# Gate products in chunks of 512, 512 and 152 columns, dt weights' two parts side by side, sample state products in four row groups

## The chip, the cores and the metric

The kernel runs on one core of a Trainium2 chip. The metric is the device time of one execution in microseconds. Engines are named as in the profile: PE is TensorE (PEld its weight loads), DVE is VectorE, ACT is ScalarE, POOL is GpSimd, SP is SyncE, which issues the transfers. TensorE multiplies a moving operand by a stationary one of up to 128 x 128 (the contraction lies on the partitions) into PSUM; the other engines evict from there.

## The reference

One inference step of a small hybrid network, in fp32, for 1024 frames of a new stream (the prompt) and 16 frames each of 8 running streams (the samples), 1152 tokens with 1024 features:

```python
def trunk(x, ...):               # for each layer, with norms before and after each part
    # layer 0: RG-LRU             layer 1: Mamba-2 SSD            each followed by SwiGLU
def rglru_mixer(...):
    r = sigmoid(xc @ w_r + b_r)  # four blocks of 256 x 256, after a causal convolution
    i = sigmoid(xc @ w_i + b_i)
def ssd_mixer(...):
    proj = h @ w_in              # z (2048), x (2048), B (512), C (512), dt (32)
    dt = softplus(dt_raw + dt_bias)
def ssd_scan(...):               # by chunk c, group g (4), head r (8 in a group)
    states = einsum('bcjgn,bcjgrp->bcgrpn', B, xdt * decay)
    s = s * exp(acs[-1]) + states
```

Outputs are the features of all tokens and the new states: of the convolutions, of the RG-LRU, and of the SSD (for each of 8 samples and 32 heads a 64 x 128 matrix).

## The kernel before, in words

**Layout.** Features lie on the partitions and tokens in the free dimension. Tokens go in three blocks of 384 (`TB`); the last holds 256 prompt tokens and the 128 sample tokens. Weights come in units of 128 x 1024 floats (`wr`), each of which is split into a rounded high part `wh` (a cast on ScalarE to the reduced format float32r) and the rest `wl` (a subtraction on VectorE); activations are split likewise (`hl` holds both parts). A product (`mm3`, line 418) is then three float32r matmuls: high by high, high by low, low by high. `gemm` (line 424) makes 8 x 3 of them for one unit and one token block into one PSUM buffer `mm`.

**Gates.** `gate` in `lru` (line 661 on) multiplies the convolved rows, 1176 columns with the padding of the samples, by a 256 x 256 block of gate weights, for r and for i. Each row of results is made in three chunks of `QC` = 392 columns, 6 matmuls each, and evicted by a sigmoid on ScalarE.

**dt.** The dt unit has 32 weight columns, the rest of its 128 are zero. `dt_tb` (line 837) makes an ordinary gemm for each block and keeps 32 rows of it (`dtr`). `dt_prep` transposes these 32 rows in nine pieces of 128 tokens on TensorE against the identity, and goes on to the decays.

**Scan.** `core` (line 898) is a generator: for each of four groups it goes through eight prompt chunks of 128 tokens and then, as a ninth, the 128 sample tokens (`smp`). A chunk loads its columns of x, B and C (`core<-xbc`) and its cumulated decays, broadcast to all partitions (`core<-acd`), transposes x and B on TensorE into `aux` and `one`, weights the results (`xdt`, `xw`), makes decay matrices on GpSimd, ScalarE and VectorE, then the outputs `py` (eight 64-row products and eight more with the state, profile rows `aux<-core,core 128*64`), and the state's increment. For the samples eight states `sb` are read in, used by eight column-tiled products (`aux<-sb,core 128*32`), and renewed. For each sample b this is: a mask of B's 128 tokens with the 16 of the sample (`bm`, on VectorE), a full product bm x xw of 128 x 512 in plain fp32 (two instructions), `sb` times its decay on GpSimd, the addition of the product on VectorE, and a transfer out.

**What sets the order.** Every operation is first recorded by a `Recorder` in program order. It works out the latest start of each operation for a TensorE without pauses, and emits all with priorities by it; the framework's scheduler then lays out each engine's instructions by these priorities and its own estimates. One rule is added (`emit`, line 319): buffers of one kind (a tag) are taken in program order, "slot order". So a PSUM buffer that is written later in the program cannot be taken before one that is written earlier. There are four buffers of the tag `mm`, three of `aux` and one of `one`; SBUF has three of `tmp` and 17 of `row`. The scan's steps are called from between the gemms of the SSD layer (`advance`, with `RATE` 0.4: one chunk for 2.5 gemms) in the order x0 x1 x2 z0 x3 z1 z2 z3. In `core` before the change no operation uses an `mm` buffer.

All recorded instructions have line L332 in the profile, since the recorder emits them there; L335 of the changed kernel is the same line.

Of the kernel before, what the change touches and what calls it, by code (L numbers as in the profile page):

```python
# [8 lines left out]
F32 = mybir.dt.float32  # L9
# [13 lines left out]
QC = NQ // 3  # L23
# [94 lines left out]
for _n, _w in [("ident", 128), ("U", 128), ("Ub", 128), ("ones", 1), ("sm", 8)]:  # L118
    CS[_n] = (_o, _o + _w)
    _o += _w  # L120
NCS = _o

# [6 lines left out]
def lay_inputs(w):  # L129
    w = {k: np.asarray(v) for k, v in w.items()}  # L130
    x = np.concatenate([w["x_prompt"].reshape(SEQ, D), w["x_sample"].reshape(NS * LS, D)], axis=0)
    xt = np.ascontiguousarray(x.T).reshape(KD, P, T).transpose(1, 0, 2)
    wu = np.stack([lay_unit(d, w) for d in plan()])
    pv = np.zeros((P, NPV), np.float32)

    def put(n, a):
        pv[:, PV[n][0]:PV[n][1]] = a

    put("g", np.concatenate([fm(w[n][l]) for l in range(2) for n in
                             ("norm_mix_pre", "norm_mix_post", "norm_ffn_pre", "norm_ffn_post")], axis=1))  # L140
    put("lcw", fm(w["lru_conv_w"][0].T))
    put("lcb", fm(w["lru_conv_b"][0]))
    put("lbr", fm(w["lru_b_r"][0].reshape(-1)))
    put("lbi", fm(w["lru_b_i"][0].reshape(-1)))
    put("lam", fm(w["lru_lambda"][0]))
    put("lh", fm(w["state_lru_h"][0].T))
    put("scw", fm(w["ssd_conv_w"][0].T))
    put("scb", fm(w["ssd_conv_b"][0]))
    put("sd", fm(np.repeat(w["ssd_d"][0], HD)))
    put("sng", fm(w["ssd_norm"][0]))  # L150
    put("dtb", np.broadcast_to(w["ssd_dt_bias"][0], (P, NH)))
    put("alog", np.broadcast_to(w["ssd_a_log"][0], (P, NH)))
    i = np.arange(P)
    same = i[:, None] // LS == i[None, :] // LS
    up = i[:, None] <= i[None, :]
    cs = np.concatenate([np.eye(P), up, up & same, np.ones((P, 1)),
                         i[:, None] // LS == np.arange(NS)[None, :]], axis=1).astype(np.float32)
    scs = fm(w["state_ssd_conv"][0].transpose(2, 0, 1)).reshape(P, 24, 24).transpose(1, 0, 2)
    lcs = w["state_lru_conv"][0].transpose(2, 0, 1).reshape(KD, P, 24)
    s0 = w["state_ssd"][0].reshape(NS, NG, HPG * HD, NST).transpose(1, 0, 3, 2)  # L160
    return {k: np.ascontiguousarray(v) for k, v in
            dict(xt=xt, wu=wu, pv=pv, cs=cs, lcs=lcs, scs=scs, s0=s0).items()}
# [36 lines left out]
def box(a):  # L199
    """The part of its tensor that an access covers: a range of each dimension (all of it where unclear)."""  # L200
# [23 lines left out]
class Recorder:  # L224
    """Collects the instructions of a program, so that each can be issued with a priority that
    follows from when the tensor engine needs its result."""
# [42 lines left out]
    def latest_starts(self, slots):  # L269
        """When each instruction has to start at the latest for the tensor engine to run without a pause."""  # L270
# [73 lines left out]
class Trunk:  # L344
# [57 lines left out]
    def prepare(self, prep):  # L402
        nc = self.nc
        while self.n_prep < min(self.n_raw, self.n_take + prep):
            r = self.raws.pop(self.n_prep)
            h, l = self.get(self.wp, "wh", 1024, F32R, "wh"), self.get(self.wp, "wl", 1024, F32R, "wl")
            nc.scalar.copy(h, r)
            (nc.gpsimd if 1 < self.n_prep < 4 else nc.vector).tensor_tensor(out=l, in0=r, in1=h.bitcast(F32), op=SUB)
            self.preps[self.n_prep] = (h, l)
            self.n_prep += 1  # L410
# [22 lines left out]
    def split_k(self, hl, k, src, scale=None):  # L433
        """hi and lo parts of a source (times a gain per feature): hi + lo is exact."""
# [16 lines left out]
    def sumsq(self, srcs, tag, engine=None, tail=0, square=None):  # L451
        """Sum of the squares of the features, in 1 + tail parts that the tensor engine adds."""
# [23 lines left out]
    def rstd_bc(self, parts, n, tag, tail=0):  # L476
        """1 / sqrt(sum over features / n + eps) of each token, on all partitions."""
# [36 lines left out]
    def store_x(self, tb, k, xt, dst):  # L514
        """Stores the tiles up to k that fill a row."""
        if k % 3 == 2 or k == KD - 1:
            n = k % 3 + 1
            self.nc.sync.dma_start(dst[:, k + 1 - n:k + 1, tb * TB:(tb + 1) * TB],
                                   xt[k // 3][:, :n * TB].rearrange("p (k t) -> p k t", k=n))
# [4 lines left out]
    def pre_rstd(self, tb, s, tail=0):  # L524
        """1/rms of each token before a mixer: it scales the products of the unnormalised x."""
# [5 lines left out]
    def boundary(self, tb, rows, xin, gpost, gpre, xout):  # L531
        """x += norm(mixer output), and what the next mixer takes of it."""
# [34 lines left out]
    def scaled(self, out, ps, tb, lo=0, hi=TB):  # L567
        """Products times 1/rms of their tokens."""
# [61 lines left out]
    def lru(self, hn, xt):  # L630
# [31 lines left out]
        def gate(w, k):  # L662
# [5 lines left out]
            for j, m in enumerate(ms):  # L668
                r[m], i[m] = self.row(s="r"), self.row(s="i")
                for dst, o, b in ((r[m], 0, "lbr"), (i[m], 256, "lbi")):  # L670
                    for c in range(3):
                        ps = self.psm()
                        cc = slice(c * QC, (c + 1) * QC)
                        for q in range(2):
                            ws = slice(q * 512 + o + j * P, q * 512 + o + (j + 1) * P)
                            self.mm3(ps[:, :QC], wh[:, ws], wl[:, ws], xch[2 * k + q][:, cc], xcl[2 * k + q][:, cc],
                                     q == 0, q == 1)
                        order.append(A.activation(dst[:, cc], ps[:, :QC], AF.Sigmoid, bias=self.pv(b, m)))
# [158 lines left out]
    def dt_tb(self, w, hn, tb):  # L837
        if tb == 0:
            self.dtr = self.row(s="dtr")
        ps = self.gemm(w, hn[tb])  # L840
        self.scaled(self.dtr[:NH, tb * TB:(tb + 1) * TB], ps[:NH], tb)

    def dt_prep(self):
# [3 lines left out]
        pt = self.psx()  # L847
        for c in range(NT):
            nc.tensor.transpose(pt[:, c * NH:(c + 1) * NH], raw[:NH, c * P:(c + 1) * P], self.ident[:NH, :NH])
# [48 lines left out]
    def core(self, g, q5, rows):  # L898
# [5 lines left out]
        for c in range(NT):  # L904
# [11 lines left out]
            # token-major copies  # L916
# [16 lines left out]
            # decay matrices  # L933
# [24 lines left out]
            # outputs, feature-major  # L958
# [23 lines left out]
            # states  # L982
# [14 lines left out]
            else:  # L997
                for b in range(NS):
                    bm = self.tmp(P, s="bm")
                    V.tensor_scalar(out=bm, in0=btok, scalar1=self.cst("sm")[:, b:b + 1], scalar2=None, op0=MUL)  # L1000
                    pst = self.psx()
                    M.matmul(pst, bm, xw, start=True, stop=True)
                    o = b * NH + g * HPG
                    G.tensor_tensor(out=v3(sb[b]), in0=v3(sb[b]),
                                    in1=bds[:, o:o + HPG].unsqueeze(2).to_broadcast([P, HPG, HD]), op=MUL)
                    V.tensor_tensor(out=sb[b], in0=sb[b], in1=pst, op=ADD)
                    nc.sync.dma_start(self.o["ss"][g, b], sb[b])
            yield

    def ssd(self, hn, xin, xout):  # L1010
# [26 lines left out]
        def advance(n, ready):  # L1037
            """Goes on with the scan: the outputs of a chunk, and the preparation of the next."""
# [11 lines left out]
        def zs(g):  # L1050
            """Gating and norm of a group."""
# [59 lines left out]
        # output projection, half of the inner width at a time  # L1111
# [25 lines left out]
    def run(self):  # L1137
        nc = self.nc
        self.pvt = self.cp.tile([P, NPV], F32, tag="pv", name="pvt")
        self.cs = self.cp.tile([P, NCS], F32, tag="cs", name="cs")  # L1140
# [27 lines left out]
        nc.sync.dma_start(self.cs, self.i["cs"])  # L1168
# [30 lines left out]
```

## Time and profile before

| what | value |
|---|---|
| median of the runs (lowest to highest of 3) | 3118.02 us (3117.15 to 3123.07) |
| span of the profiled execution (no time of its own is listed) | 3121.6 us |
| mean granted TensorE clock | 0.981 |
| TensorE busy | 3004.5 us, 96%, 17659 instructions |
| VectorE, ScalarE, GpSimd busy | 1734.4, 1010.2 and 466.3 us |
| gate matmuls, 392 columns, three groups of 96 | 34.5 + 34.0 + 33.7 us busy |
| sample state products, 64 instructions | 34.7 us busy |
| longest wait of TensorE | 14.89 us, at 1288.73 us, on VectorE's `rs` |

The RG-LRU layer takes the span's first 446 us, the first SwiGLU runs to about 1290, the SSD layer to about 2200, the second SwiGLU to the end. A row of the timeline gives start, duration, engine, line, operation, written and read tile, shapes and count, and in brackets the idle time of the engine before it with what ended it. In a row of groups the shape behind a tile's names is the stationary operand's and then the moving one's. Durations of matmuls overlap: the next starts before the last has ended, so that TensorE's time for one is read from start to start.

### The profile page before, as it was taken

Reading aid. Unit: us, or ns where it says so; the run is one execution under the profiler, and the core shown is the slowest. Engines: PE = TensorE matmul, PEld = TensorE weight load, DVE = VectorE, ACT = ScalarE, POOL = GpSimd, SP = SyncE. Lnnn points to the kernel's source line nnn. Section 1 sums busy time; section 2 is a strip of 40 time slices with the busy share of each in tenths; the row PEclk is TensorE's granted clock in tenths of the full one; section 3 lists DMA queues with packets and bytes.
Section 4 is the critical chain, followed back from the end, with each engine's and each line's share of the span. In section 5 each row is a group of like instructions: output and inputs, shape, how many; then the busy total and the mean of one; then the engine's idle time right before and its main releaser. Section 6 shows DMA issues by size and latency. Waiting matters only on the chain. (4 is left out here: it accounts for less than half of the span.)

```text
span 3121.6 us, 42961 instructions
## 1 busy us (share of the span) xinstructions
PE 3004.5 (96%) x17659; PEld 2920.9 (94%) x17659; DVE 1734.4 (56%) x2948; ACT 1010.2 (32%) x1477; POOL 466.3 (15%) x468
## 2 busy tenths in 40 slices
PE   7999989999999999799999999999999999999997
PEld 7999989999999999798887978899999999999997
DVE  7765282444444445867876867642662444444446
ACT  4774343111111112445554545232333111111111
POOL 4210230000000001314443432100220000000003
PEclk9999999999999999899999999999999999999998
DMA  3111231111111112335563644622221111111113
GB/s 122 43 42 41 83 107 48 46 43 41 41 41 41 41 44 74 107 120 177 164 184 122 205 161 128 238 99 101 80 88 43 47 41 41 41 48 41 41 36 120
DMA packets 176036, 263.21 MB, mean 84 GB/s; under 512 B 19136, under 2 KB 130112, under 8 KB 175840
## 3 DMA queue, kind: packets, MB, share of 16 engines
q1 hardware_dynamic: 175840, 260.47, 25.4%
q8 instruction: 139, 2.28, 0.3%
q14 instruction: 57, 0.47, 0.0%
HBM read 198.46 MB, written 61.97 MB: 83 GB/s over the span
## 5 line engine op out<-in xcount | busy, mean ns | idle before, releaser
L332 PE MATMUL mm<-hl,wh 128*128 128x384 f32 x7728 | 1992.7, 338 | 13.2 <-ACT hl L332 6.3
L332 PEld LDWEIGHTS mm<-hl,wh 128*128 128x128 f32 x7728 | 1404.8, 189 | 32.3 <-issue 13.2
L332 PE MATMUL mm<-hl,wl 128*128 128x384 f32 x3864 | 1296.1, 338 | 1.8 <-DVE wl L332 1.8
L332 PEld LDWEIGHTS mm<-hl,wl 128*128 128x128 f32 x3864 | 730.3, 189 | 8.1 <-issue 5.6
L332 ACT CAST wh<-wr 128x1024 fp32r<-128x1024 f32 (+1 forms) x218 | 227.9, 1046 | 760.1 <-PE mm L332 753.1
L332 DVE TENSOR_TENSOR acc<-acc,mm 128x384 f32<-128x384 f32 x504 | 274.5, 552 | 213.3 <-PE mm L332 211.5
L332 DVE TENSOR_TENSOR wl<-wr,wh 128x1024 fp32r<-128x1024 f32 (+1 forms) x216 | 269.2, 1247 | 190.5 <-ACT wh L332 190.5
L332 PE MATMUL mm<-ah,wh 128*128 128x384 f32 x1056 | 356.0, 338 | 1.7 <-DVE acc L332 0.9
L332 POOL TENSOR_TENSOR npost<-npost,npost 128x384 f32<-128x384 f32 x65 | 70.3, 1081 | 1915.5 <-ACT npost L332 1913.6
L332 PE MATMUL mm<-al,wh 128*128 128x384 f32 x1056 | 355.2, 337 | 1.0 <-DVE al L332 1.0
L332 PE MATMUL mm<-ah,wl 128*128 128x384 f32 x1056 | 353.6, 336 | 0.0
L332 DVE TENSOR_TENSOR silu<-silu,mm 128x384 f32<-128x384 f32 x132 | 72.9, 554 | 373.2 <-PE mm L332 370.8
L332 PEld LDWEIGHTS mm<-ah,wh 128*128 128x128 f32 x1056 | 198.1, 188 | 2.5 <-DVE acc L332 1.4
L332 PEld LDWEIGHTS mm<-al,wh 128*128 128x128 f32 x1056 | 198.2, 188 | 1.3 <-DVE al L332 1.3
L332 PEld LDWEIGHTS mm<-ah,wl 128*128 128x128 f32 x1056 | 198.1, 188 | 0.0
L332 DVE TENSOR_TENSOR silu<-mm,rstd 128x384 f32<-128x384 f32 x132 | 73.2, 557 | 221.4 <-PE mm L332 215.7
L332 ACT CAST ah<-silu 128x384 fp32r<-128x384 f32 x132 | 67.8, 514 | 361.4 <-DVE silu L332 361.4
L332 DVE SCALAR_TENSOR_TENSOR xc<-pad,pvt,xc 128x1176 f32<-128x1176 f32 x96 | 148.3, 1552 | 21.7 <-ACT xc L332 21.1
L332 ACT ACTIVATE silu<-silu 128x384 f32<-128x384 f32 x132 | 68.8, 523 | 269.7 <-DVE silu L332 269.7
L332 ACT ACTIVATE core<-core 128x1024 f32<-128x1024 f32 x100 | 102.5, 1053 | 103.0 <-POOL core L332 102.7
L332 DVE TENSOR_TENSOR core<-core,core 128x1024 f32<-128x1024 f32 x64 | 95.4, 1491 | 64.1 <-ACT core L332 38.8
L332 ACT ACT_TABLE_LOAD x86 | 110.3, 1283 | 56.2 <-DVE z L332 24.5
(147 smaller groups left out, 2664.3 us busy)
## 6 DMA issues: line engine op xcount, KB each, us to landing
wr<-in_wu SPq DMA_DIRECT2D x216, 512.0 KB, 3.5
core<-acd SPq DMA_DIRECT2D x36, 512.0 KB, 5.2
xbc<-pad SPq DMA_DIRECT2D x24, 576.0 KB, 3.5
core<-xbc SPq DMA_DIRECT2D x36, 384.0 KB, 3.9
xs<-x SPq DMA_DIRECT2D x18, 576.0 KB, 3.0
x<-xs SPq DMA_DIRECT2D x18, 576.0 KB, 5.4
ysc<-core SPq DMA_DIRECT2D x36, 256.0 KB, 3.5
y<-ysc SPq DMA_DIRECT2D x16, 576.0 KB, 5.4
```

The lines of the kernel that those rows point to most:

```text
L332: op.ins = getattr(getattr(self.nc, op.engine), op.name)(*op.args, **op.kw).ins
```

## The change

Three edits; the removal of comments is left out.

Gates: the 1176 columns go in chunks of 512, 512 and 152.

dt: in the dt unit's `wh` tile the high parts stand in columns 0 to 31 and the low parts in columns 32 to 63, and there is no `wl`. A block then needs two matmuls for each of eight pieces, one for each part of the activations. The two sets of 32 rows are added when the rows are transposed: the identity is replaced by a 64 x 32 matrix `two`, which is loaded into a `tmp` buffer, with a plain fp32 product.

States: two masks instead of eight, one with the odd and one with the even samples. Under a mask a group of 32 tokens (partitions) has just one sample left, so its product needs a contraction over 32 rows only. Four such products go to four row groups of the array, into two `aux` and two `mm` buffers. The multiplication by the decay, the addition and the transfer follow as before, with the four samples of a mask together.

```diff
-QC = NQ // 3
+QCS = ((0, 512), (512, 1024), (1024, NQ))
...
-for _n, _w in [("ident", 128), ("U", 128), ("Ub", 128), ("ones", 1), ("sm", 8)]:
+for _n, _w in [("ident", 128), ("U", 128), ("Ub", 128), ("ones", 1), ("sm", 8), ("odd", 2), ("two", 32)]:
...
-                         i[:, None] // LS == np.arange(NS)[None, :]], axis=1).astype(np.float32)
+                         i[:, None] // LS == np.arange(NS)[None, :],
+                         i[:, None] // LS % 2 == np.arange(2)[None, :],
+                         i[:, None] % NH == np.arange(NH)[None, :]], axis=1).astype(np.float32)
...
+            h = self.get(self.wp, "wh", 1024, F32R, "wh")
+            if self.units[self.n_prep] == ("dt",):
+                v = r.rearrange("p (k c) -> p k c", k=KD)
+                hv = h.rearrange("p (k c) -> p k c", k=KD)
+                nc.scalar.copy(hv[:, :, :NH], v[:, :, :NH])
+                nc.scalar.copy(hv[:, :, 2 * NH:], v[:, :, 2 * NH:])
+                nc.vector.tensor_tensor(out=hv[:, :, NH:2 * NH], in0=v[:, :, :NH], in1=hv[:, :, :NH].bitcast(F32), op=SUB)
+                self.preps[self.n_prep] = (h, None)
...
-                    for c in range(3):
-                        ps = self.psm()
-                        cc = slice(c * QC, (c + 1) * QC)
+                    for c0, c1 in QCS:
+                        ps = self.psm()[:, :c1 - c0]
+                        cc = slice(c0, c1)
...
-        ps = self.gemm(w, hn[tb])
-        self.scaled(self.dtr[:NH, tb * TB:(tb + 1) * TB], ps[:NH], tb)
+        ps = self.psm()
+        wh, (rh, rl) = w[0], hn[tb]
+        for k in range(KD):
+            ws, rs = slice(k * P, (k + 1) * P), slice(k * TB, (k + 1) * TB)
+            self.nc.tensor.matmul(ps[:, :TB], wh[:, ws], rh[:, rs], start=k == 0, stop=False)
+            self.nc.tensor.matmul(ps[:, :TB], wh[:, ws], rl[:, rs], start=False, stop=k == KD - 1)
+        self.scaled(self.dtr[:2 * NH, tb * TB:(tb + 1) * TB], ps[:2 * NH], tb)
...
+        two = self.tmp(NH, s="two")
+        nc.sync.dma_start(two, self.i["cs"][:, NCK:])
         for c in range(NT):
-            nc.tensor.transpose(pt[:, c * NH:(c + 1) * NH], raw[:NH, c * P:(c + 1) * P], self.ident[:NH, :NH])
+            nc.tensor.matmul(pt[:, c * NH:(c + 1) * NH], raw[:2 * NH, c * P:(c + 1) * P], two[:2 * NH],
+                             start=True, stop=True)
...
-                for b in range(NS):
+                for j in range(2):
                     bm = self.tmp(P, s="bm")
-                    V.tensor_scalar(out=bm, in0=btok, scalar1=self.cst("sm")[:, b:b + 1], scalar2=None, op0=MUL)
-                    pst = self.psx()
-                    M.matmul(pst, bm, xw, start=True, stop=True)
-                    o = b * NH + g * HPG
-                    G.tensor_tensor(out=v3(sb[b]), in0=v3(sb[b]),
-                                    in1=bds[:, o:o + HPG].unsqueeze(2).to_broadcast([P, HPG, HD]), op=MUL)
-                    V.tensor_tensor(out=sb[b], in0=sb[b], in1=pst, op=ADD)
-                    nc.sync.dma_start(self.o["ss"][g, b], sb[b])
+                    V.tensor_scalar(out=bm, in0=btok, scalar1=self.cst("odd")[:, j:j + 1], scalar2=None, op0=MUL)
+                    pst = [self.psx() for _ in range(2)] + [self.psm() for _ in range(2)]
+                    for q in range(4):
+                        r = slice(q * 32, (q + 1) * 32)
+                        M.matmul(pst[q], bm[r], xw[r], start=True, stop=True)
+                    for q in range(4):
+                        b = 2 * q + j
+                        o = b * NH + g * HPG
+                        G.tensor_tensor(out=v3(sb[b]), in0=v3(sb[b]),
+                                        in1=bds[:, o:o + HPG].unsqueeze(2).to_broadcast([P, HPG, HD]), op=MUL)
+                        V.tensor_tensor(out=sb[b], in0=sb[b], in1=pst[q], op=ADD)
+                        nc.sync.dma_start(self.o["ss"][g, b], sb[b])
```

The scheduler lays out the SSD layer anew. Three places of TensorE's order in group 0 of the scan follow. A row gives line, operation, the written tile with its buffer's number, the read tiles, and the shape of the result; `mm` rows with `hl` are gemm matmuls, `aux_1483` and `aux_1496` the outputs of prompt chunks 6 and 7 (`py`), `aux_1515` those of the samples.

In the kernel before, from the state's increment of chunk 6 on:

```order
L332 MATMUL aux_1484<-core_1396,core_1392 128x512
L332 MATMUL aux_1485<-cs,core_1393 128x128 x4
L332 MATMUL one_1486<-cs,core_1393 128x128
L332 MATMUL one_1486<-core_1393 128x128
L332 MATMUL mm_1535<-hl_1313,wh_1491 128x384 x2
L332 MATMUL mm_1535<-hl_1313,wl_1492 128x384
L332 MATMUL mm_1535<-hl_1313,wh_1491 128x384 x2
```

Gemm matmuls of `mm_1535` and `mm_1547` go on, 33 in all, up to the first row of `aux_1496`. They belong to gemms that come later in the program than the sample's states.

In the changed kernel, from the same instruction on:

```order
L335 MATMUL aux_1484<-core_1396,core_1392 128x512
L335 MATMUL aux_1485<-cs,core_1393 128x128 x4
L335 MATMUL one_1486<-cs,core_1393 128x128
L335 MATMUL one_1486<-core_1393 128x128
L335 MATMUL aux_1496<-core_1399,core_1396 64x128 x2
L335 MATMUL aux_1496<-core_1395,core_1397 64x128 x2
```

The outputs of chunk 7 follow at once. The last gemm ahead of here is `mm_1513`, the next in the program behind the states is `mm_1528`, which is also the next in the order.

The sample's products in the changed kernel (`bm_1516` and `bm_1521` are the two masks; of the first, `aux_1517` is row group 0, `aux_1518` row group 1, `mm_1519` and `mm_1520` row groups 2 and 3; of the second `aux_1522`, `aux_1523`, `mm_1524` and `mm_1525` likewise):

```order
L335 MATMUL aux_1515<-core_1398,core_1396 64x128 x2
L335 MATMUL aux_1517<-core_1396,bm_1516 128x512
L335 MATMUL mm_1519<-core_1396,bm_1516 128x512
L335 MATMUL mm_1520<-core_1396,bm_1516 128x512
L335 MATMUL mm_1524<-core_1396,bm_1521 128x512
L335 MATMUL mm_1525<-core_1396,bm_1521 128x512
L335 MATMUL aux_1515<-cs,core_1394 128x128
```

Where before a single product stood behind the first outputs of the sample, five now stand there; `aux_1518` and `aux_1522` come behind the rest of the outputs, and `aux_1523` among the gemm matmuls of `mm_1528`.

More of the change, by code (lines that the diff above doesn't have):

```diff
@@ L121 @@
 NCS = _o
+NCK = CS["two"][0]
 def fm(v):
@@ L405, in prepare @@
             r = self.raws.pop(self.n_prep)
-            h, l = self.get(self.wp, "wh", 1024, F32R, "wh"), self.get(self.wp, "wl", 1024, F32R, "wl")
+            h = self.get(self.wp, "wh", 1024, F32R, "wh")
[6 more added lines that the diff above has]
+                self.preps[self.n_prep] = (h, None)
+                self.n_prep += 1
+                continue
+            l = self.get(self.wp, "wl", 1024, F32R, "wl")
             nc.scalar.copy(h, r)
@@ L670, in gate @@
                 for dst, o, b in ((r[m], 0, "lbr"), (i[m], 256, "lbi")):
-                    for c in range(3):
-                        ps = self.psm()
-                        cc = slice(c * QC, (c + 1) * QC)
+                    for c0, c1 in QCS:
+                        ps = self.psm()[:, :c1 - c0]
+                        cc = slice(c0, c1)
                         for q in range(2):
                             ws = slice(q * 512 + o + j * P, q * 512 + o + (j + 1) * P)
-                            self.mm3(ps[:, :QC], wh[:, ws], wl[:, ws], xch[2 * k + q][:, cc], xcl[2 * k + q][:, cc],
+                            self.mm3(ps, wh[:, ws], wl[:, ws], xch[2 * k + q][:, cc], xcl[2 * k + q][:, cc],
                                      q == 0, q == 1)
-                        order.append(A.activation(dst[:, cc], ps[:, :QC], AF.Sigmoid, bias=self.pv(b, m)))
+                        order.append(A.activation(dst[:, cc], ps, AF.Sigmoid, bias=self.pv(b, m)))
                 V.tensor_tensor(out=xcs[m][:, n], in0=xcs[m][:, n], in1=i[m][:, n], op=MUL)
@@ L1139, in run @@
         self.pvt = self.cp.tile([P, NPV], F32, tag="pv", name="pvt")
-        self.cs = self.cp.tile([P, NCS], F32, tag="cs", name="cs")
+        self.cs = self.cp.tile([P, NCK], F32, tag="cs", name="cs")
         self.ident, self.ones = self.cst("ident"), self.cst("ones")
@@ L1167, in run @@
         nc.sync.dma_start(self.pvt[:, 64:], self.i["pv"][:, 64:])
-        nc.sync.dma_start(self.cs, self.i["cs"])
+        nc.sync.dma_start(self.cs, self.i["cs"][:, :NCK])
         hn = [self.split([self.xk(xt[0], k) for k in range(KD)], 0)]
```

## The prediction

> **What bounds the kernel now.** I read the page first, then TensorE's waits, then its timeline around the three edited places. From the page, the span, the busy times and the granted clock in 40 slices:
>
> ```profile
> span 3121.6 us, 42961 instructions
> PE 3004.5 (96%) x17659; PEld 2920.9 (94%) x17659; DVE 1734.4 (56%) x2948; ACT 1010.2 (32%) x1477; POOL 466.3 (15%) x468
> PEclk9999999999999999899999999999999999999998
> ```
>
> TensorE is busy for 96% of the span at nearly full clock, so a matmul that is taken out is worth its start-to-start time wherever TensorE does not wait. It is idle for 117 us (3121.6 less 3004.5). What it waits for, in total, times and longest:
>
> ```profile
> PE aux L332 <- DVE rs L332: 25.7, 6, 14.9
> PE aux L332 <- DVE core L332: 17.2, 10, 3.8
> PE one L332 <- DVE rs L332: 13.4, 3, 7.9
> PE aux L332 <- DMA core<-xbc: 7.3, 6, 2.7
> ```
>
> The `rs` waits are the norms between layers, which nothing here touches. The `core` and `xbc` waits belong to the scan, from 1400 to 2000 us, and there the edit of the states lies. So two questions set the answer: how many TensorE slots go, and what the scan's waits become.
>
> The sum is made against the profiled execution, 3121.6 us of span, which lies 3.6 us above the median of the runs (3118.0) and inside their range; I subtract those 3.6 at the end. What this kernel's measurement can tell from no change is 0.2%, 6.2 us.
>
> **Gates.** The instructions keep number and order; of each three chunks of 392 columns two become 512 wide and one 152. On TensorE's timeline the first gate matmul, and the first row behind 72 of them:
>
> ```profile
> 85.13 0.34 PE L332 MATMUL mm<-xch,wh 128*128 128x392 f32 x1
> 97.99 0.51 PE L332 MATMUL mm<-hl,wh 128*128 128x384 f32 x2
> 1459.18 0.60 PE L332 MATMUL aux<-cs,core 128*128 128x128 f32 x4
> 1459.62 0.27 PE L332 MATMUL one<-cs,core 128*128 128x128 f32 x1
> ```
>
> 12.86 us over 72 is 0.179 us for 392 columns, 0.536 for three. By proportion 512 columns take 0.233. No hi/lo (f32r) matmul under 384 columns is in this trace, so the 152-wide one is bounded: 0.069 by proportion; 0.110 if it cannot go below what a 128-wide one with a full weight load takes (the last two rows: four in 0.44 us); and 0.254 if narrow f32r falls to the rate of plain fp32, which the products below show as 0.857 us for 512 columns. Three chunks then take 0.536, 0.577 or 0.721, and the 96 triples 0, +3.9 or +17.8 us. I take +3.9: a 128-wide matmul is nearest in width, and it has the same 128 weight columns to load. ScalarE's 72 sigmoid evictions cover the same columns in the same number of instructions: nothing.
>
> **dt.** Each token block issues 16 matmuls for 24, so 24 go. A 384-wide one takes 0.173 us (fifteen lie between the first two rows below, 2.60 us), so 4.2 us. But the first block's eight stand ahead of the wait in the third row:
>
> ```profile
> 1510.96 0.51 PE L332 MATMUL mm<-hl,wh 128*128 128x384 f32 x2
> 1513.56 0.51 PE L332 MATMUL mm<-hl,wh 128*128 128x384 f32 x2
> 1288.73 1.65 PE L332 MATMUL aux<-cs,rs 128*128 128x128 f32 x6 [14.89 <-DVE rs L332]
> L332 PE MATMUL aux<-cs,dtr 32*128 32x32 f32 x9 | 0.9, 227 | 0.0
> ```
>
> TensorE waits 14.9 us for VectorE there, and 1.4 us less work in front only makes the wait longer. That leaves −2.8. The nine transposes become nine fp32 products of two instructions each, in four clusters instead of two by the order: nine more instructions at about 0.11 and two more changes of tile shape at about 0.1 (both from rows of the neighbouring parts), +1.2. Sum −1.6, bounds −4.2 and 0. The weight unit's preparation gets shorter on ScalarE and VectorE; the one new transfer on SP's queue and its `tmp` slot stand long ahead of their use. Nothing.
>
> **Sample products.** Before, eight full products in a group. The timeline gives one product with one gemm matmul behind it, and the column-tiled products of the same width:
>
> ```profile
> 1530.80 1.02 PE L332 MATMUL aux<-core,bm 128*128 128x512 f32 x2
> 1531.25 0.74 PE L332 MATMUL mm<-hl,wl 128*128 128x384 f32 x1
> 1531.83 0.51 PE L332 MATMUL mm<-hl,wh 128*128 128x384 f32 x2
> 1508.38 0.34 PE L332 MATMUL mm<-hl,wh 128*128 128x384 f32 x1
> 1508.65 1.93 PE L332 MATMUL aux<-sb,core 128*32 128x512 f32 x16
> 1510.50 0.44 PE L332 MATMUL mm<-hl,wh 128*128 128x384 f32 x1
> ```
>
> 1.03 us less 0.173 is 0.857 for a product, 6.86 for a group's eight. The eight column-tiled ones take 1.85 us together, less than a third of 6.86, so four column groups do run side by side; entering the tiled shape costs 0.27 − 0.173, some 0.1 us. Row groups of 32 never stand side by side in this trace. If they overlap as column groups do, what counts is which stand next to each other: the order does not keep the eight in two fours, but in runs such as q0 q2 q3, q2' q3', q1 q0', q1', where two of one row group follow each other serially. That is four slots for eight, 3.43 us and 0.5 for the changes of shape, −2.9 us a group. If they do not overlap: +0.5 a group.
>
> [...]
>
> In group 0 I count the gain as nothing, since TensorE waits around these products (next part). Groups 1 to 3: −8.7; bounds −11.7 and +2.
>
> VectorE's masks fall from 32 to 8:
>
> ```profile
> L332 DVE TENSOR_SCALAR bm<-core,cs 128x128 f32<-128x128 f32 x32 | 18.5, 595 | 0.0
> L332 POOL TENSOR_TENSOR sb<-sb,bds 128x512 f32<-128x512 f32 x32 | 41.2, 1320 | 1.6 <-PE aux L332 1.6
> L332 DVE TENSOR_TENSOR sb<-sb,aux 128x512 f32<-128x512 f32 x32 | 21.7, 681 | 6.7 <-PE aux L332 6.2 <-issue 0.3
> ```
>
> That is 13.9 us of VectorE, spread over four places; I price it at nothing, because the gemm evictions beside it are not waited for, and at −3 at best.
>
> **Cover lost in group 0.** This is the largest term. Half of the products now take `mm` buffers, and buffers of one kind are taken in program order, so a gemm written behind the products may not start before them. Before, gemms that are written later ran ahead between the outputs of the prompt's last chunks. The order counts 54, 33, 16 and 19 gemm matmuls between the outputs of chunks 5, 6, 7, the sample's state reads, and its outputs; of the change it counts 21, 0, 0, 0. So 101 of 122 leave this stretch, 17.5 us at 0.173. What TensorE did there before, with VectorE at chunk 6, and the group of the convolution's passes:
>
> ```profile
> L332 DVE SCALAR_TENSOR_TENSOR xc<-pad,pvt,xc 128x1176 f32<-128x1176 f32 x96 | 148.3, 1552 | 21.7 <-ACT xc L332 21.1
> 1477.18 3.02 PE L332 MATMUL aux<-core,core 128*64 128x128 f32 x34
> 1491.84 3.02 PE L332 MATMUL aux<-core,core 128*64 128x128 f32 x34 [1.47 <-DVE core L332]
> 1501.29 3.02 PE L332 MATMUL aux<-core,core 128*64 128x128 f32 x34
> 1504.95 0.63 PE L332 MATMUL aux<-cs,core 128*128 128x128 f32 x4 [0.64 <-DMA core<-xbc]
> 1515.32 1.13 PE L332 MATMUL aux<-core,bm 128*128 128x512 f32 x2 [0.88 <-POOL core L332]
> 1486.51 1.91 DVE L332 SCALAR_TENSOR_TENSOR xc<-pad,pvt,xc 128x1176 f32<-128x1176 f32 x1
> 1488.54 2.02 DVE L332 SCALAR_TENSOR_TENSOR xc<-pad,pvt,xc 128x1176 f32<-128x1176 f32 x1
> 1490.48 1.21 DVE L332 TENSOR_TENSOR core<-core,core 128x1024 f32<-128x1024 f32 x1
> ```
>
> Even with its cover TensorE waited at chunk 6, at the sample's transposes and at its first product: there VectorE, a transfer and GpSimd end last, and taking matmuls from ahead of them lengthens the wait one for one. At chunk 6: 1.47 and 33 × 0.173 = 7.2 us. The other 68 matmuls stood ahead of points with some slack; following the chain of transfers, ScalarE's exponentials and VectorE's products through the new order, I put 7 to 10 of their 11.8 us as wait. So 13 to 16 up to the sample's outputs. Upper bound 17.5; lower bound: the convolution's `xc` passes, which stand ahead of the chain's product on VectorE (the last three rows), belong to such gemms; if eight of them move off too, the chain is 8 × 1.55 = 12.4 us shorter, which leaves 5.
>
> Behind the sample's outputs the quads hold all four `mm` buffers and two of three `aux`. The next gemm, and with it everything behind it on TensorE, waits for GpSimd's third multiplication and VectorE's addition, 3 × 1.32 + 0.68 = 4.6 us, of which the sample's outputs, as long as a chunk's 3.0, cover the most part. The next group's transposes wait for their transfer, which starts when the chunk's row is read out, later than before by that. 3 to 10 us, taken as 6. Together +20, bounds 5 and 27.
>
> [...]
>
> **Cover gained in group 1, and the clock.** The 101 gemm matmuls run later: between the outputs of group 1's chunks the order counts 376 before and 503 now. TensorE waited there, and the clock fell behind the waits (start, busy; and span, busy times, PEclk):
>
> ```profile
> 1590.91 0.87 PE L332 MATMUL aux<-cs,core 128*128 128x128 f32 x4 [2.71 <-DMA core<-xbc]
> 1640.68 0.44 PE L332 MATMUL aux<-core,core 128*64 128x128 f32 x4 [2.33 <-DVE core L332]
> 1648.36 0.49 PE L332 MATMUL aux<-cs,core 128*128 128x128 f32 x2 [2.88 <-DVE core L332]
> 1702.96 0.83 PE L332 MATMUL aux<-cs,ssq 128*128 128x1 f32 x6 [3.04 <-DVE ssq L332]
> 1590.00:1597.00 7.00, 6.08 (x29) 6.12 (x30) 6.03 (x11) 4.20 (x6) 0.01 (x1) 0.76 0.65 162
> 1648.00:1655.00 7.00, 6.64 (x24) 3.69 (x25) 3.36 (x8) 0.00 (x0) 3.60 (x4) 0.58 0.28 93
> 1702.00:1709.00 7.00, 6.04 (x27) 6.04 (x28) 5.81 (x28) 0.53 (x1) 0.00 (x0) 0.63 0.24 75
> ```
>
> With 14 more gemm matmuls (2.4 us) ahead of each of nine chunks the first three waits, 7.9 us, can go, and two clock dips of 7 us × (1 − 0.76) and (1 − 0.58), 4.6 us: −12.5 at best, −4 at least; I take −9.5. In turn the new waits of group 0 are as long as those that were followed by a dip, 7 × (1 − 0.63) = 2.6 each: two, +5, bounds 0 and +8.
>
> **Sum.** +3.9 − 1.6 − 8.7 + 20 − 9.5 + 5 = +9.1 us, 3130.7 for the profiled execution, 3127 for the median of runs. Slower by 0.3%.
>
> **Rivals.**
> Faster: VectorE catches up. With the gemms their convolutions leave group 0, and the chain shortens with the cover. For it: the `xc` rows stand directly ahead of the product at 1490.48; against it: the waits at the transposes and the first product end on a transfer and on GpSimd. With the lower bound of the cover term, 5, and one dip saved the sum is 9.1 − 15 − 2.6 = −8.5: 3109.5. With one dip fewer it decides below a cover term of some 7 us; from there to 17 us the sum stays within 0.2%.
> The narrow chunk at fp32's rate: +17.8 for +3.9, 3141. For it: other fp32 work here pays that rate; against it: 384 and 392 columns show no fixed part.
> The row groups do not overlap, so the change doesn't do what it says on the chip: +0.5 for −2.9 in groups 1 to 3, +10.2, 3137.
> The terms cancel: cover 11 instead of 20, 3118.
>
> **How the numbers follow.** The forecast (order as read, floor at the weight load, overlap): 0.34. Faster: 0.26. Narrow chunk: 0.14. No overlap: 0.08. Cancel: 0.18. Predicted: 3127 us. The likeliest case's own range is 3122 to 3136; with the others the range is 3104 to 3144. Faster by over 0.2% has the faster case, 0.26. Within 0.2%: the cancel case and a part of the forecast, 0.22. Slower: the rest, 0.52.
>
> **What would show it.** Gates: the 152-wide rows' start-to-start, 0.07, 0.11 or 0.25 us. Products: whether `aux<-core,bm` and `mm<-core,bm` of different row groups start within a few ns of each other. Cover: TensorE's waits between the outputs of chunk 5 and group 1's first transposes, about 24 us for about 4; under 10 and I am wrong on the largest term. Group 1: waits on `core` under 3 us. dt: the wait on `rs` near 16 us for 14.9.

## The result and the profile after

The changed kernel takes 3142.06 us in the median of its runs (3138.78 to 3147.15), the kernel before 3118.11: a ratio of 1.0077, 95% interval 1.0060 to 1.0094. It is slower by 24 us. The profiled execution took 3138.8 us, the shortest of the four, with a span of 3136.9 us. The spans of the two profiled executions differ by only 15.3 us, since that of the kernel before lies above its median.

From the page of the changed kernel, and from its list of what TensorE waited for (in total, times, longest):

```profile
span 3136.9 us, 42901 instructions
PE 3010.1 (96%) x17644; PEld 2915.3 (93%) x17644; DVE 1723.3 (55%) x2924; ACT 1008.8 (32%) x1478; POOL 468.7 (15%) x468
```

```profile
PE aux L335 <- DVE rs L335: 27.2, 6, 16.3
PE aux L335 <- DVE core L335: 19.1, 7, 7.1
PE aux L335 <- DMA core<-xbc: 11.2, 4, 6.1
PE aux L335 <- POOL core L335: 3.4, 1, 3.4
PE mm L335 <- DVE sb L335: 3.3, 1, 3.3
```

The waits of the norms (`rs`) are the old ones. In the scan the longest on VectorE's `core` is 7.1 us for 3.8, the one on GpSimd's `core` 3.4 for 0.9, and one is new: a gemm that wants an `mm` buffer waits for VectorE's `sb`, since a state product holds that buffer. TensorE has 15 instructions fewer and is busy longer, which points to the clock. TensorE in group 0 of the scan, from the outputs of chunk 6 to the sample's first products, in the timeline of the changed kernel:

```profile
1489.29 5.42 PE L335 MATMUL aux<-core,core 128*64 128x128 f32 x34 [7.09 <-DVE core L335]
1497.79 4.64 PE L335 MATMUL aux<-core,core 128*64 128x128 f32 x34 [2.31 <-DVE core L335]
1506.10 0.44 PE L335 MATMUL aux<-core,core 128*64 128x128 f32 x4 [0.86 <-DVE core L335]
1509.98 1.22 PE L335 MATMUL aux<-core,bm 32*128 32x512 f32 x1 [3.44 <-POOL core L335]
1509.99 1.22 PE L335 MATMUL mm<-core,bm 32*128 32x512 f32 x2
```

The first wait, 1.47 us before, is 7.09 now; the outputs of chunk 6 take 5.42 us for 3.02, since the clock is halved behind the wait (0.50 from 1488 to 1494 us, 0.78 in the mean from 1484 to 1507 us). The last two rows show three row groups that start within 10 ns: they do run side by side. Busy times and, in the third column from the end, the granted clock in three stretches of group 0, of the changed kernel and then of the kernel before:

```profile
1467.00:1507.00 40.00, 29.28 (x210) 23.61 (x208) 28.67 (x47) 17.52 (x22) 16.38 (x16) 0.87 0.56 170
1508.00:1525.00 17.00, 15.02 (x48) 9.10 (x49) 7.32 (x12) 2.95 (x3) 11.49 (x11) 0.50 0.49 160
1526.00:1534.00 8.00, 6.27 (x36) 5.39 (x35) 4.10 (x5) 2.39 (x3) 1.36 (x2) 1.00 0.58 181
```

```profile
1470.00:1507.00 37.00, 34.89 (x260) 31.73 (x259) 31.62 (x47) 20.55 (x25) 19.56 (x20) 1.00 0.58 169
1508.00:1525.00 17.00, 16.12 (x93) 11.15 (x92) 11.04 (x23) 5.43 (x6) 11.90 (x10) 1.00 0.61 184
```

For 17 us around the sample's products the clock stands at one half, although TensorE is busy for 15 of them. I call **lost clock** the span times what the mean granted clock lacks to 1; each run states both. It is 82 us in the mean of the change's runs and 59 to 64 us in those of the kernel before beside the runs below. Behind the dt products (from 1368 us on) the profiled executions have 10.1 us more idle time of TensorE up to the last matmul (53.7 and 63.8) and 23.6 us more lost clock (35.3 and 58.9); the rest, −16.9, is work that went and lost clock that fell on idle time.

### The profile page after: what moved, and what is told of

It is laid out like the page before. It is cut to its first block, busy times and chain, and to the rows that moved or that the text cites. A ratio compares the mean times of both kernels' runs of the same rounds, so it can differ in the third digit from the quotient of the medians.

```text
span 3136.9 us, 42901 instructions
## 1 busy us (share of the span) xinstructions
PE 3010.1 (96%) x17644; PEld 2915.3 (93%) x17644; DVE 1723.3 (55%) x2924; ACT 1008.8 (32%) x1478; POOL 468.7 (15%) x468
## 3 DMA queue, kind: packets, MB, share of 16 engines
q8 instruction: 139, 2.28, 0.3%
## 5 line engine op out<-in xcount | busy, mean ns | idle before, releaser
L335 PE MATMUL mm<-hl,wh 128*128 128x384 f32 x7728 | 1989.7, 339 | 15.7 <-ACT hl L335 6.1
L335 ACT CAST wh<-wr 128x1024 fp32r<-128x1024 f32 (+2 forms) x219 | 227.7, 1041 | 771.9 <-PE mm L335 764.2
L335 PE MATMUL aux<-core,core 128*64 128x128 f32 (+1 forms) x1088 | 111.1, 318 | 17.5 <-DVE core L335 10.7
```

The lines of the kernel that those rows point to most:

```text
L335: op.ins = getattr(getattr(self.nc, op.engine), op.name)(*op.args, **op.kw).ins
```

## Experiments

Theory ("cover"): the loss comes from the states' edit, because its `mm` buffers hold back the gemms that stood between the scan's outputs. Rivals: the other two edits cost their share; the row-group products themselves cost, by the clock or by their shape. The times are medians; the ratio is to the kernel before, run beside.

### One edit at a time

**Gates alone** (the kernel before with `QCS`):

> Only the gate chunks are changed (512, 512, 152); the order of every engine's work is that of the kernel before. The cover theory (the loss comes from the sample states' edit) expects no change, within 0.1%: the changed kernel was 0.4 us ahead of the kernel before at its last gate matmul. If the gates' own price decides, 96 triples at 0.575 us for 0.536 give +3.7 us, 3122; a narrow chunk at plain fp32's rate would give +17 us.

3132.0 us, 1.0041 (1.0027 to 1.0055): neither. One premise was false: the order isn't that of the kernel before. The instructions of the SSD layer are the same, but the scheduler lays them out by its own estimates, and with other gate durations it laid out group 0 anew: 35, 42, 24 and 24 gemm matmuls between the outputs for 54, 33, 16 and 19. Up to the dt products the trace is only 0.2 us further behind than it was at the first gate. The loss arises from there on, as 7.1 us more idle time ahead of chunk 5 of group 0 (14.0 for 6.9), with no more lost clock (59.4 us in the mean). So this run prices a layout, not the gates.

**dt alone**, and **gates and dt together** (the change with the states' edit undone):

> Only the dt edit. Both theories expect a small gain: 16 gemm matmuls of 0.173 us that do not end in the wait on rs (2.8 us) less about 1.2 us for the two-instruction products: -1.6 us, 3116.5, within 0.1% of before. If the added products or the new transfer cost more than that, it is above 3118.

> The changed kernel with the sample states' products as before: gates and dt together. The cover theory expects the loss gone and dt's gain kept: -1 to -2 us, 3116 to 3117. If the edits disturb one another, it differs from the sum of the two single edits by more than 2 us.

dt: 3118.6 us, 1.0002 (0.9994 to 1.0011). Both: 3119.4 us, 1.0005 (0.9996 to 1.0015). No change, and none between the two. Here both kernels have the order of the kernel before in the scan, so the gates themselves cost nothing that can be measured.

**States alone** (the kernel before with the third edit):

> Only the sample states' edit; gates and dt as before. The cover theory expects all of the loss here, and a little more than in the whole change since dt's gain is missing: ratio 1.008, 3142 to 3146 us, with about 15 us of TensorE idle time and a mean clock near 0.82 in group 0 between the outputs of chunk 5 and the next group's first transposes. If the three edits share the loss, it is nearer to 1.004.

3144.9 us, 1.0089 (1.0076 to 1.0103), with 82 us of lost clock in the mean: all of the loss, as the theory said. Its idle time in group 0 is 14.1 us, its clock there 0.88 rather than 0.82.

### Buffers without row groups

```diff
-                    pst = self.psx()
+                    pst = self.psx() if b % 4 < 2 else self.psm()
```

> The kernel before with eight masks and eight full 128-row products as it had them; only, half of the products are written into mm buffers instead of aux. No row groups, gates and dt as before. By the order the gemm matmuls between group 0's outputs fall to 21, 0, 0, 0, as in the change. The cover theory expects it to be slow without any row group: 3140 to 3160, with group 0's idle time near 15 us and the clock near 0.8. If the row groups are what costs, it stays at 3118 within 5 us.

3141.9 us, 1.0070 (1.0057 to 1.0083). The kernel before with nothing but half of its products in `mm` is as slow as the change. Its waits in group 0, in the timeline, are those of the change (7.09, 2.31) to within 0.2 us; the third falls on the sample's transposes:

```profile
1488.84 5.10 PE L332 MATMUL aux<-core,core 128*64 128x128 f32 x34 [7.20 <-DVE core L332]
1497.01 3.02 PE L332 MATMUL aux<-core,core 128*64 128x128 f32 x34 [2.30 <-DVE core L332]
1503.13 0.79 PE L332 MATMUL aux<-cs,core 128*128 128x128 f32 x4 [3.09 <-DMA core<-xbc]
```

Elsewhere the gemms queue behind products in `mm` buffers that wait for their masks on VectorE, 7.0 us at the longest. No row group is in this kernel: the buffers are enough for the loss. That doesn't yet say that row groups are free, since its products also take 11.7 us more of TensorE's time (of its slots) than those of the change were thought to.

### Group 0 as before

The change, but with group 0's states made as before (the old block for group 0, the new one for the others):

> The changed kernel, but group 0's sample products as before (eight full products in aux buffers); groups 1 to 3 in four row groups with mm buffers. The cover theory, with all of the loss in group 0, expects 3108 to 3120. If the loss comes as much from the clock dips of groups 1 to 3 (0.94 of full clock from 1729 to 2034 us of the change, 0.97 before), it is 3124 to 3134.

3132.5 us, 1.0042 (1.0030 to 1.0054): the second case. With group 0 untouched more than half of the loss is still there, and in the profile it shows around the products of the later groups. Between 1530 and 1700 us the kernel before has a clock of 0.97 (first row), this one 0.94 (second), with a half-clock stretch at group 1's products (third):

```profile
1530.00:1700.00 170.00, 161.02 (x1055) 141.02 (x1055) 125.85 (x186) 92.81 (x112) 66.48 (x59) 0.97 0.54 168
```

```profile
1530.00:1700.00 170.00, 159.50 (x1040) 138.18 (x1039) 118.67 (x176) 89.69 (x107) 67.30 (x59) 0.94 0.53 165
1637.00:1654.00 17.00, 13.91 (x43) 6.88 (x42) 12.37 (x18) 7.96 (x8) 11.93 (x9) 0.51 0.30 94
```

### Work for nothing in the waits

```diff
             py = self.psx()
+            for _ in range({6: 10, 7: 4, 8: 2}.get(c, 0) if g == 0 else 0):
+                M.matmul(py[:, :384], self.cst("U"), self.cs[:, :384], start=True, stop=True)
```

> The changed kernel with sixteen extra plain fp32 products of constants (128 x 384, some 0.64 us each, 10.3 us) that stand in group 0 in front of the outputs of chunk 6 (ten), chunk 7 (four) and the samples (two) and are overwritten: work for nothing, set where TensorE waits. If the clock dips cost time of their own (13.6 us of lost clock in group 0 of the change), the dips shrink and the time falls to 3130 to 3138 for the change's 3142. If the dips only fall on time that is lost anyway, the time stays or grows by up to 10 us.

3141.3 us, 1.0072 (1.0058 to 1.0087): between the two cases, level with the change. In its profile group 0's lost clock falls from 13.7 to 2.4 us and its idle time from 15.4 to 7.8. So 10 us of extra work cost nothing, and won nothing: by this, a dip that lies on a chain that is waited for anyway isn't worth its full length, though the profiled execution is the shortest of four, 8 us under their median. It doesn't tell the two apart further. One thing in this profile counts for what follows: the eight products of group 0, in row groups as in the change, here come together, from 1512.51 to 1515.53 us, and the clock is full while they run (the two instructions of a product start 0.54 us apart, for 1.01 in the change); a stretch of 3.4 us at half follows only at 1521 us.

### Row groups without the buffers

The change with three `aux` buffers and the buffer `one` for a mask's products:

```diff
-                    pst = [self.psx() for _ in range(2)] + [self.psm() for _ in range(2)]
+                    pst = [self.psx() for _ in range(3)] + [self.psx("one")]
```

> The changed kernel, but the four row-group products of a mask go into three aux buffers and the buffer one instead of two aux and two mm; no product holds an mm buffer. By the order the gemm matmuls between group 0's outputs are 54, 33, 16, 15 again (54, 33, 16, 19 before; 21, 0, 0, 0 in the change). The cover theory expects the loss gone: TensorE idle in group 0 near 4 us, clock near 1.0 there, 3108 to 3120 (the products' gain of up to 8.7 us only as far as row groups stand next to each other). If the row-group products themselves lower the clock or block TensorE, it stays above 3130.

3135.0 us, 1.0049 (1.0032 to 1.0066): the cover theory alone missed. The gemms are back between group 0's outputs and its idle time from chunk 5 to group 1 is 3.4 us (3.8 in the kernel before), yet the time stays up, with 75 us of lost clock for 60 beside it. The scheduler set the eight products one by one or in pairs between gemms. At group 0's products TensorE had waited just 1.1 us, and then the clock was halved for 16 us in which TensorE was never idle:

```profile
1507.00:1515.00 8.00, 6.89 (x43) 4.54 (x41) 4.32 (x9) 3.29 (x5) 3.59 (x3) 1.00 0.60 170
1516.00:1532.00 16.00, 16.00 (x45) 9.17 (x44) 6.37 (x11) 3.83 (x4) 9.19 (x8) 0.50 0.55 188
1533.00:1540.00 7.00, 7.00 (x36) 5.20 (x37) 5.74 (x10) 2.59 (x3) 1.63 (x4) 1.00 0.63 173
```

So a second theory was needed, "low load", a guess from this stretch: products over 32 rows count as little use of the array, and the clock goes down.

The kernel before with 32-row products, one at a time, in nearly its own order:

```diff
-                    M.matmul(pst, bm, xw, start=True, stop=True)
+                    r = slice(b // 2 * 32, b // 2 * 32 + 32)
+                    M.matmul(pst, bm[r], xw[r], start=True, stop=True)
```

> The kernel before, with its eight masks, its aux buffers and nearly its order of work (73 of 12432 rows of TensorE's order differ); only, each sample product contracts over its own 32 rows instead of 128, one product at a time as before. Theory 'low load': TensorE's clock is halved in windows in which the array is little used, and products over 32 rows count as little use; it expects new half-clock windows at the products and 3121 to 3130, with at least 6 us more lost clock between 1370 and 2010 us than the 20 us before. Theory 'waits only' (dips follow idle time): no change, 3118 within 4 us, lost clock near 20 us.

3131.7 us, 1.0032 (1.0019 to 1.0045), with 6.9 ± 4.0 us more lost clock than beside it (the bounds here and below are two standard errors): above the range's top in the median, and slower as low load said. But the profile shows another cost too. One product among gemm matmuls:

```profile
1518.11 0.34 PE L332 MATMUL mm<-hl,wh 128*128 128x384 f32 x1
1518.37 1.12 PE L332 MATMUL aux<-core,bm 32*128 32x512 f32 x2
1519.42 0.44 PE L332 MATMUL mm<-hl,wh 128*128 128x384 f32 x1
1519.71 0.34 PE L332 MATMUL mm<-hl,wl 128*128 128x384 f32 x1
```

1.60 us from the first row to the last, for a product and two matmuls of 0.173: 1.25 us for the product and its two changes of shape, where the full one takes 0.857. That is 0.4 us each and 12.8 us for all 32, of which the waits swallow a part. In this one profile, the shortest but one of nine runs, only 3.4 us more clock are lost from 1370 to 2010 us than in the kernel before (23.9 for 20.5), where low load asked for 6, and most of the scan's half-clock stretches don't lie at the products; the lost clock is shown by the runs' means, its place here is not.

The change with 128-row products in its buffers and nearly its order:

```diff
-                        M.matmul(pst[q], bm[r], xw[r], start=True, stop=True)
+                        M.matmul(pst[q], bm, xw, start=True, stop=True)
```

> The changed kernel with its two masks, its buffers and nearly its order; only, each of the eight products contracts over all 128 rows (so it adds up the four samples of a mask, and the states it writes are not the samples' own). No two can run side by side: eight slots of 0.857 us for about four in each group, +11.7 us in all if nothing else changes. Theory 'low load' expects the half-clock windows at groups 0 and 1's products (17.1 and 13.7 us in the change) to shrink to 7 us or less and the lost clock from 1370 to 2010 us to fall by 10 us or more from 42.6, so that the time is 3135 to 3146 for the change's 3142. Theory 'waits only' expects the windows to stay and 3150 to 3156.

3137.6 us, 1.0056 (1.0044 to 1.0068): "waits only" falls. 11.7 us of product slots were to come on top of the change's 3142, and the time is if anything lower. The waits ahead are still there (7.35, 2.31, 2.49 us), but around the products the clock is 0.96 for the change's 0.50, and the lost clock from 1370 to 2030 us is 25.6 us for 42.7:

```profile
1508.00:1525.00 17.00, 15.43 (x75) 8.74 (x66) 9.45 (x16) 2.95 (x3) 14.18 (x11) 0.96 0.52 169
```

### Fours undivided

Three `aux` and `one` again, and each mask is made only when all four buffers are free. The line that holds the masks back (the comment is added here, the lines that collect `yo` and `adds` are left out):

```diff
+                    mk.after += adds if j else [yo]   # mk: the mask; yo: last eviction of py; adds: of the first four
```

> The changed kernel with the four products of a mask in three aux buffers and the buffer one (no mm), and with each mask made only when all four buffers are free (the first behind the evictions of the sample's outputs, the second behind the additions of the first four), so that the four products of a mask become ready together; by the order all eight fours then stand undivided, and the gemm matmuls between group 0's outputs are 54, 33, 16, 15. If the loss comes from the cover and from row-group products that stand apart (0.4 us each more than a full product between gemms, and low load), both are gone: a four takes some 1.25 us with its changes of shape for 3.43 before, 8 fours -17 us, so 3100 to 3112. If row-group products lower the clock in any arrangement, lost clock of 5 to 15 us is added and it is 3112 to 3127.

3116.9 us, 0.9996 (0.9987 to 1.0005): 25 us under the change and level with the kernel before; above the range of the first case, within that of the second. A four in the timeline:

```profile
1525.64 0.51 PE L335 MATMUL mm<-hl,wh 128*128 128x384 f32 x2
1526.08 0.71 PE L335 MATMUL aux<-core,bm 32*128 32x512 f32 x3
1526.10 0.69 PE L335 MATMUL one<-core,bm 32*128 32x512 f32 x1
1526.61 0.60 PE L335 MATMUL aux<-core,bm 32*128 32x512 f32 x3
1526.63 0.59 PE L335 MATMUL one<-core,bm 32*128 32x512 f32 x1
1527.15 0.44 PE L335 MATMUL mm<-hl,wl 128*128 128x384 f32 x1
```

1.07 us from the first product to the next gemm matmul, 1.25 with the changes of shape. The same kernel with 128-row products (the diff of the change with full rows, above):

> The kernel of the run e11 (fours undivided, in three aux buffers and one), but each product contracts over all 128 rows, so no two run side by side (it adds up the four samples of a mask; the states it writes are not the samples' own). By the order its groups 0 and 1 are laid out as in e11, groups 2 and 3 a little differently. If undivided fours pay what their slots say, eight fours take 3.43 us each instead of 1.25 and the time is 17 us above e11's 3117, 3130 to 3136. If row groups lose as much to the clock as they save, it stays within 5 us of 3117.

```profile
1522.25 2.74 PE L335 MATMUL aux<-core,bm 128*128 128x512 f32 x6
1524.83 1.02 PE L335 MATMUL one<-core,bm 128*128 128x512 f32 x2
```

3116.9 us, 0.9998 (0.9988 to 1.0007): the second case. Three full products take 2.58 us up to the fourth, 0.86 each, and a full four 3.43, so eight fours of row groups save 17 us of TensorE's time, and none of it is left in the end. The lost clock takes 9 us of it back (65.1 us for 56.1 in the means of eleven runs each, ± 3.4), and in the two profiles, which differ a little in groups 2 and 3, the idle time takes 7 (119.6 us of the span for 112.3): between 1368 and 2040 us TensorE waits 13.9 us for VectorE's `core` instead of 9.5, and 13.1 us for the scan's loads instead of 10.3. From 1500 to 2000 us, with row groups and then with full rows:

```profile
1500.00:2000.00 500.00, 465.08 (x3084) 414.39 (x3083) 370.97 (x634) 249.29 (x303) 196.76 (x169) 0.96 0.54 175
```

```profile
1500.00:2000.00 500.00, 471.04 (x3069) 413.11 (x3068) 367.01 (x626) 245.15 (x300) 192.34 (x167) 0.98 0.54 175
```

Low load alone doesn't say where the clock goes: in the profile of the row-group fours no half-clock stretch meets any of the 32 products. Around the eight of group 0:

```profile
1520.00:1540.00 20.00, 19.80 (x121) 17.34 (x120) 18.17 (x26) 8.70 (x10) 13.55 (x13) 1.00 0.59 196
```

No version that was tried is faster than the kernel before beyond its uncertainty.

## Why the prediction was right, and where it was short

The direction and the range held: slower was forecast, 3127 with a range of 3104 to 3144, and 3142 was measured. The mechanism that was given the largest term is the one that the runs show to be enough for the loss. That the range held is in part luck: 3142 lies above the likeliest case's own range (3122 to 3136), and the range reached up to 3144 because of a narrow chunk at fp32's rate (3141) and of row groups that don't overlap (3137), neither of which came. The sum was 15 us short of the median, with errors both ways: the gates and the lost cover were put too high, the products, group 1 and the clock too favourably. The steps:

**Gates.** The price of the narrow matmul was right, but at the gates the edit cost nothing. In the changed kernel's timeline the narrow chunk's instructions stand 0.11 us apart, at the floor that was taken from 128-wide matmuls:

```profile
98.10 0.28 PE L335 MATMUL mm<-xcl,wh 128*128 128x152 f32 x1
98.21 0.27 PE L335 MATMUL mm<-xch,wl 128*128 128x152 f32 x1
98.32 0.28 PE L335 MATMUL mm<-xch,wh 128*128 128x152 f32 x1
```

The 512-wide take 0.231, so 96 triples cost 3.7 us more, +3.9 in the sum. But from the first to the last gate matmul the changed kernel gains 0.2 us. With 392 columns two waits of 2.19 and 1.18 us near 208 us were followed by a dip of the clock (0.94 from 160 to 222 us); with the wide chunks the same waits, 2.28 and 0.97, were not (1.00):

```profile
160.00:222.00 62.00, 57.78 (x308) 56.29 (x308) 39.33 (x41) 44.06 (x53) 9.01 (x14) 0.94 0.14 44
```

```profile
160.00:222.00 62.00, 58.36 (x318) 52.97 (x317) 40.76 (x43) 44.18 (x54) 10.21 (x15) 1.00 0.14 44
```

All five profiled kernels with 392 columns have this dip (with dt alone the clock is 0.94 there too), of the nine with wide chunks two (with gates and dt it is 1.00); why the others escape it isn't shown. The rival of a narrow chunk at fp32's rate is out.

**dt.** The first block's matmuls did end in the wait, 16.3 us for 14.9, as said. The net of −1.6 is below what the runs resolve: 1.0002 (0.9994 to 1.0011).

**Sample products.** That row groups overlap was right; the rival of no overlap is out. The term of −8.7 us failed. The slots were priced at 0.857 us as for full products; a set of row groups side by side, and a lone product too, takes 1.05 to 1.07 us, with its two changes of shape 1.25, so that 16 sets cost some 20 us of the 27.4 rather than 15.7 with the changes of shape. And a saved slot was taken as time saved in groups 1 to 3. The last pair of runs shows that not even eight undivided fours, 17 us, shorten the kernel.

**Cover lost.** The first step was right to a tenth: 7.2 us at chunk 6 was forecast, 7.09 came, and 7.20 where only the buffers were changed. Of the 7 to 10 us at the other points 2.31, 0.86, 3.44 and, at the next group's transposes, 1.73 came. As idle time of group 0 that makes +11.6 us (3.8 to 15.4), not +20. Of the eight convolution passes on which the faster rival counted, three left the stretch with the gemms (VectorE's at 1500.98 and 1506.35 us of the kernel before, 5.9 us), none of them ahead of chunk 6, where the wait came as forecast; that is a part of the difference.

**Cover gained in group 1, and the clock.** These two terms failed. Group 1 was to give back 9.5 us; its idle time went from 8.8 to 8.5 us and its lost clock from 5.1 to 8.5, as I read it because group 1's own products hold back the gemms in turn: the kernel with group 0 as before still lost 13 us. The loss was placed in one group, but the samples' products bring it in the later ones too. The clock was priced as two dips of 2.6 us, at most 8; 22 us more are lost between 1370 and 2030 us. The prediction had dips only behind idle time. In three pairs of kernels with 32-row and 128-row products in nearly the same arrangement, those with 32 rows lose more clock in the means of their runs (7, 12 and 9 us; the two kernels of the 12 were not run side by side). Long half-clock stretches at the products themselves stand only where the products are broken up among other work (17 us at 0.50 in the change, 16 us with three `aux` and `one`); in the kernel with undivided fours all of them ran at full clock (1.00 from 1520 to 1540 us, around group 0's). So the means show that kernels with 32-row products lose more clock; by which mechanism stays open.

In the traces of the kernel before and of the changed kernel every half-clock stretch of the scan lasts 3.4, 6.8, 13.7 or 17.1 us. That products over 32 rows bring on such stretches fits the means above, and is argued, not shown.

So the buffers alone are enough for most or all of the 24 us (+22 with the buffers alone, +17 with the change's order and full rows). But row groups broken up without any `mm` buffer cost 16 us too, so the two don't add up, and a share of each in the 24 can't be given. Row groups, which were to give 8.7 back, gave nothing, and in the change's broken arrangement they cost at least what they save.

## What to carry to other kernels

When instructions move to another pool of buffers, ask which work waits for that pool in program order: a few products in the matmul pool stopped the gemms that had filled the scan's waits, and cost 22 us with the buffers alone, more than every slot that they could save (17 us). Undivided sets of row-group products need buffers that nothing else waits for and one event that makes all of them ready, and even then gained nothing here (3116.9 us with them and with full products); set apart between full matmuls each costs more than a full product (1.25 us for 0.857). A saved slot is worth its time only where TensorE is the last to finish, and a schedule that is computed from a model may shift far from the edit, so an edit is priced only beside a run whose order is the same.

## What the runs showed of the hardware

- Four fp32 products of 32 rows and 512 columns in four row groups start within 0.02 us of one another and take 1.07 us together up to the next full matmul, 1.25 with both changes of shape; a full product takes 0.857, four of them 3.43.
- A single such product between full matmuls costs 1.25 us with its two changes of shape, 0.4 more than the full one.
- With 32-row products the granted clock was halved for 16 us while TensorE had no idle time at all. With 128-row products in the same buffers and order it was 0.96 in the place where it was 0.50. With 32-row products in undivided fours no half-clock stretch met them (1.00 from 1520 to 1540 us, around the first eight).
- A float32r matmul of 152 columns takes 0.11 us from start to start, the time of one of 128 fp32 columns (four in 0.44); 512 columns take 0.231.
- Around a wait of 2.2 to 2.3 us between gate matmuls, near 208 us, the clock was halved for 3.4 or 6.8 us in five kernels of five with 392-column chunks and in two of nine with 512-column chunks.
